# Identity matrix and norm weights loaded ahead of x, and the sums of squares of five norms issued behind the scaled values

## The chip, the cores and the metric

The kernel runs on one core of a Trainium2 chip. The core has a matrix engine (TensorE, PE in the profile), three engines for elementwise work (VectorE or DVE, ScalarE or ACT, GpSimd or POOL) and SyncE (SP), which issues most transfers. Each engine runs its own instructions in order, and an instruction whose input or whose buffer is not ready holds up everything behind it on that engine. The metric is the device time of one execution in microseconds (us), as the median of several runs. Three runs of the kernel before took 1461.05, 1462.23 and 1462.77 us, so its median is 1462.23 us.

## The reference

The program is a decoder trunk of two layers over 256 positions of width 1024, with batch 1.

```python
def rmsnorm(x, g):
    y = xf * lax.rsqrt(jnp.mean(xf * xf, axis=-1, keepdims=True) + EPS) * g
```

Layer 0 normalizes x and multiplies it by one combined input weight. The columns of the product feed a short gated convolution and a gated DeltaNet, which is computed in chunks:

```python
    log_a = -jnp.exp(A_log) * jax.nn.softplus(af + dt_bias)
    beta = jax.nn.sigmoid(bf)
    gc = jnp.cumsum(g, axis=-1)
    decay = jnp.where(tril, jnp.exp(jnp.where(tril, diff, 0.0)), 0.0)
    A = jnp.where(strict, jnp.einsum('bhncd,bhnjd->bhncj', kb, kc) * decay, 0.0)
    M = A + jnp.eye(C)
    u = lax.linalg.triangular_solve(M, vb, left_side=True, lower=True, unit_diagonal=True)
```

After the mixer come an output projection and a residual add, then a dense SwiGLU (width 2816) with its own norm, then a gated embedding add with a norm. Layer 1 is built alike, with differential attention and a convolution module as mixers, and 8 experts (top 2) in place of the dense SwiGLU. A last norm ends it.

## The kernel before

All activations of a layer stand transposed in on-chip memory: 8 tiles of 128 features by 256 positions. Each product is done in pieces: a value v is held as a high part (`..h`, rounded for the fast matrix path) and a low part (`..l`, what the rounding left), and a product of two such values is three matmuls. For weights, SP loads a raw tile (`r_..`), ACT casts it to the high part (`h_..`, L145), and DVE subtracts to get the low part (`l_..`, L146). The casts write into a few buffers in rotation, so a cast waits until the matmuls that used its buffer are done.

A norm is done late: `late_norm_T` (L257) transposes h on PE (`nt_..`, L249), ACT scales each transposed piece by the norm's weight (`x_..h`, L200), DVE makes the low part (`x_..l`, L201). The factor 1/rms of each position is left out there. It is worked out beside it: four `Square` activations per norm with a sum as second output (`sum_sq`, L227; tile `jk_..`), then some small DVE operations (`rsqrt`, L213 to L218; `rq..`), and it is applied to the results of the projection.

The layer-0 mixer runs in this order of use. `in_og` is the projection that gives the output gate and the two small gate inputs af and bf, from four loads of 2 k-tiles each, 96 matmuls of 260 columns. `in_k`, `in_q`, `in_v` (96 matmuls of 256 columns each), `in_cg` and `in_x` follow. From af and bf come beta and the log decay g, by exponentials on ACT and a row of small DVE operations. g goes through a cumulative sum on PE (`pcs`), its exponential (`ec`) and the decay matrices (`pd`, `dec`, and their transposes `pdt`). The key side gives `pk`, and with it the chunk matrices A0 and A1 (one for each half of the positions). Their triangular inverse is built by doubling: `Ti` is set up on DVE, `put` transposes it on PE, ACT copies that to `U`, and then each of six levels does for each half a product `p1`, a masked copy `Ym` on DVE, a product `p2`, an update of U on DVE, a transpose `p3` and a copy to Ti on ACT.

Which instruction stands where on each engine is not the order of the source. A list scheduler goes over the program and lays out each engine's order by its own estimates of times, and it keeps dependences, buffers and the edges that the source sets with `tc.issue_after`. A small edit to the source can thus move instructions far away. The helper `after(*names)` sets such an edge: everything in its block is issued after the named last instruction on its engine; `last["high"]` is the last ACT instruction that made a high part in `split` (L195).

Transfers at the start: SP issues half 0 of x and then the identity (64 KB of `cst`), ACT issues half 1 of x and then the norm weights and other columns (`prm`, 122 KB), and POOL issues a broadcast row of parameters (`row`, L422) and the rest of the constants. Behind its two, SP goes on with the weights, `r_in_og` first.

Of the kernel before, what the change touches and what calls it, by code (L numbers as in the profile page):

```python
# [16 lines left out]
P = 128  # L17
D = 1024
T = 256
NB = 2  # L20
# [63 lines left out]
def trunk_kernel(  # L84
# [3 lines left out]
    ple_w_proj, ple_w_gate, prm_in, row_in, cst_in, oh_in, out, stage=99,  # L88
):
    nc = tc.nc  # L90
    pe, act, dve, pool, sync = nc.tensor, nc.scalar, nc.vector, nc.gpsimd, nc.sync
# [22 lines left out]
    xv = x.rearrange("o (b p) d -> p (o b) d", p=P)  # L114
    cst = cp.tile([P, C_L0], F32, name="cst")
    prm = cp.tile([P, N_COL], F32, name="prm")
    sync.dma_start(h[:, 0, :], xv[:, 0, :])
    act.dma_start(h[:, 1, :], xv[:, 1, :])
    sync.dma_start(cst[:, 0:P], cst_in[:, 0:P])
    act.dma_start(prm, prm_in)  # L120
    ident = cst[:, C_ID : C_ID + P]
    stU = cst[:, C_STU : C_STU + P]
    iota = cst[:, C_IO : C_IO + P]
# [28 lines left out]
    def after(*names):  # L152

        stack = ExitStack()
        for n in names:
            stack.enter_context(tc.issue_after(last[n].ins))
        return stack
# [33 lines left out]
    def parts(shape, tag, name, pool_, bufs=1):  # L191
        return (pool_.tile(shape, F32R, tag=tag + "h", name=name + "h", bufs=bufs),
                pool_.tile(shape, F32R, tag=tag + "l", name=name + "l", bufs=bufs))
# [31 lines left out]
    def sum_sq(ss, name, b, i):  # L225
        junk = s2(f"jk_{name}{b}{i}", [P, 512])
        act.activation(junk, h[:, b, HALF[i]], AF.Square, accum_out=ss[:, i : i + 1])  # L227

    def inv_root(ss, name, n):

        m = gp.tile([P, n], F32, tag=f"ms{n}", name=f"ms_{name}", bufs=2)
        ss = ss.rearrange("q (b i) -> q b i", i=2)
        dve.tensor_tensor(m, ss[:, :, 0], ss[:, :, 1], ADD)
        dve.tensor_scalar(m, m, 1.0 / D, EPS, MUL, ADD)
        return rsqrt(m, n)

    def inv_rms(name, b):

        ss = gp.tile([P, 2], F32, tag="ss", name=f"ss_{name}{b}", bufs=2)
        for i in range(2):  # L240
            sum_sq(ss, name, b, i)
        return inv_root(ss, f"{name}{b}", 1)
# [9 lines left out]
    def gained(xT, gname, k):  # L252
        q = transpose_h(gname, k)
        for j in range(2):
            split(sub2(xT, slice(None), k + j), q[:, j, :], scale=pcol(gname[:3], 8 * int(gname[3]) + k + j))

    def late_norm_T(gname):  # L257


        xT = parts([P, KT, T], "xT", f"x_{gname}", gp, bufs=XT_BUFS)  # L260
        for k in range(0, KT, 2):
            gained(xT, gname, k)
        return xT, [inv_rms(gname, b) for b in range(NB)]

    def halves_norm_T(gname):

# [124 lines left out]
    def ple(i, o, tail=None, mark="", norm=None):  # L391

        xT, r = norm or late_norm_T(f"ple{i}{mark}")
        pieces = LAST_PIECES if tail else PIECES
        pins = {2: [(f"ple{i}", 0, "high"), (f"ple{i}", 0, "low")]} if norm else {}
        banks = proj4(ple_w_gate[i], of(xT), f"pg{i}{mark}", (0, 2), (4,), pieces, pins)

        order = pieces if tail else sorted(pieces)
        gate = {}

        def sigmoid(j):
            if j < len(order):
                b, c, n = order[j]
                gate[j] = s2(f"pg{i}{b}{c}{mark}", [P, n])
                last["sigmoid"] = act.activation(gate[j], banks[b, c], AF.Sigmoid, scale=r[b])

        sigmoid(0)
        for j, (b, c, n) in enumerate(order):
            sigmoid(j + 1)
            g, s = gate[j], slice(c % 512, c % 512 + n)  # L410
            dve.tensor_tensor(g, g, o[b][c // 512][:, s], MUL)
            to = g if tail else h[:, b, c : c + n]
            dve.tensor_tensor(to, g, h[:, b, c : c + n], ADD)
            if tail:
                tail(to, b, c, n)


    def layer0_mixer():
        with tc.tile_pool(name="l0", bufs=1) as lp:
# [16 lines left out]
            def col4(t):  # L436
                return t[:, :, None].to_broadcast([P, 4, P])

            xT, r = late_norm_T("mix0")
            rB, rB2 = spread(r, "mix0")  # L440
            yT = parts([P, KT, T], "xT", "y0", gp, bufs=XT_BUFS)
# [250 lines left out]
    def layer0_ffn():  # L692
        with tc.tile_pool(name="ffn", bufs=1) as lp:
# [4 lines left out]
            for b, n in BLOCKS:  # L698
                copy(b, n)
            xT, r = late_norm_T("ffn0")  # L700
            rB, rB2 = spread(r, "ffn0")
            nt = DFF // P
# [853 lines left out]
```

## Time and profile before

| what | value |
|---|---|
| median of three runs | 1462.23 us (1461.05 to 1462.77) |
| the profiled execution | 1461.34 us |
| span of that execution, first to last instruction | 1459.5 us |
| mean granted clock of TensorE | 0.995 |
| PE busy | 1420.2 us, 97% of the span |
| weight loads of PE | 1202.9 us, 82% |
| DVE busy | 1255.2 us, 86% |
| ACT busy | 1059.0 us, 73% |

The profiled execution took 1.84 us more than its span, and 0.89 us less than the median of the runs. PE is busy nearly all the time, so a gap in its work is what to look for: it has one of 8 us at the start, one of 2 us behind the first transposes, and later ones mostly well under 1 us. Busy time of PE is summed from matmuls whose ends are modelled, and its instructions overlap, so the start times tell more than the lengths. In the rows below, the number in brackets at the end is the engine's idle time before the group, with the engine and instruction that ended it. The numbers behind the tile names are left out by the page, so `p` is p1, p2 or p3, told apart by what they read.

### The profile page before, as it was taken

What the parts mean: (1) busy time and instruction counts of PE and PEld (TensorE: products, weight loads), DVE (VectorE), ACT (ScalarE), POOL (GpSimd) and SP (SyncE); (2) the same over time, 40 slices, a digit from 0 to 9 for tenths busy, and PEclk for the clock granted to TensorE, in tenths of its full rate; (3) what the DMA queues carried; (4) which work ended last, traced back from release to release, by engine and by line L of the source; (5) the groups of instructions that cost most, each with busy time, mean ns of one, the idle gap of its engine ahead of it and who ended that gap; (6) DMA issues with size and microseconds to landing.
All of it is one profiled execution on the core that took longest, in us unless ns stands there. A gap on an engine that the chain in (4) does not pass through costs nothing.

```text
span 1459.5 us, 21991 instructions
## 1 busy us (share of the span) xinstructions
PE 1420.2 (97%) x7726; PEld 1202.9 (82%) x7726; DVE 1255.2 (86%) x1716; ACT 1059.0 (73%) x1441; POOL 5.0 (0%) x14
## 2 busy tenths in 40 slices
PE   7999999999999999999999999999999999999996
PEld 6999899988897888888888678888778888778755
DVE  6868655545789599999999999899999899999997
ACT  6545544446646578898888879788888788888875
POOL 0000000000000000000000000000000000000000
PEclk9999999999999999999999999999999999999998
DMA  9604666555461539999999999999999999999990
GB/s 351 219 8 126 200 197 194 180 186 196 144 200 55 203 110 414 369 375 406 384 401 408 411 382 383 394 371 412 405 414 411 404 369 413 406 410 404 382 340 32
DMA packets 137762, 440.36 MB, mean 302 GB/s; under 512 B 9195, under 2 KB 34316, under 8 KB 123564
## 3 DMA queue, kind: packets, MB, share of 16 engines
q1 hardware_dynamic: 133536, 434.24, 78.3%
q10 hardware_dynamic: 3724, 3.36, 0.7%
q0 software_dynamic: 384, 1.29, 0.3%
q8 instruction: 62, 1.02, 0.3%
q14 instruction: 56, 0.46, 0.1%
HBM read 435.97 MB, written 2.88 MB: 301 GB/s over the span
## 4 chain that ended last, share of the span: by engine, by line
PE 80%; DVE 11%; ACT 4%; issue 3%; DMA 2%; ACTq 0%; POOL 0%; DVEq 0%; POOLq 0%
PE mg L174 16%; PE mu L174 16%; PE y L174 14%; PE fu L174 4%; PE fg L174 4%; PE fd L174 4%; PE mt L174 3%; DVE l L146 3%; PE wo L174 3%; DVE l_d L146 2%; PE pg L174 2%; PE p L174 1%; DVE cc L842 1%; PE in_og L174 1%; PE xg L174 1%
## 5 line engine op out<-in xcount | busy, mean ns | idle before, releaser
L146 DVE TENSOR_TENSOR l<-r_gu,h 128x1024 fp32r<-128x1024 f32 x448 | 518.1, 1218 | 7.7 <-ACT h L145 5.3
L145 ACT CAST h<-r_gu 128x1024 fp32r<-128x1024 f32 x448 | 446.5, 1055 | 30.7 <-PE mu L174 11.7
L146 DVE TENSOR_TENSOR l_d<-r_d,h_d 128x1024 fp32r<-128x1024 f32 x220 | 256.0, 1218 | 11.9 <-ACT h_d L145 11.2
L145 ACT CAST h_d<-r_d 128x1024 fp32r<-128x1024 f32 x220 | 220.2, 1060 | 10.0 <-PE mu L174 4.4
L146 DVE TENSOR_TENSOR l_gu<-r_gu,h_gu 128x1024 fp32r<-128x1024 f32 x44 | 53.8, 1224 | 48.0 <-ACT h_gu L145 48.0
L145 ACT CAST h_gu<-r_gu 128x1024 fp32r<-128x1024 f32 x44 | 46.0, 1049 | 63.8 <-PE fu L174 45.4
L174 PE MATMUL y<-l_d,mh 128*128 128x512 f32 x216 | 70.6, 408 | 2.3 <-DVE l_d L146 2.2
L174 PE MATMUL y<-l_d,mhh 128*128 128x512 f32 x224 | 70.5, 396 | 0.5
L174 PE MATMUL y<-h_d,mhh 128*128 128x512 f32 x224 | 69.5, 391 | 0.0
L174 PE MATMUL y<-h_d,mhl 128*128 128x512 f32 x224 | 69.1, 390 | 0.0
L174 PE MATMUL y<-h_d,mh 128*128 128x512 f32 x216 | 66.9, 391 | 1.3 <-DVE mh L198 1.3
L174 PEld LDWEIGHTS y<-l_d,mh 128*128 128x128 f32 x216 | 37.7, 188 | 21.3 <-DVE l_d L146 15.7
L146 DVE TENSOR_TENSOR l_fd<-r_fd,h_fd 128x1024 fp32r<-128x1024 f32 x22 | 27.0, 1225 | 29.4 <-ACT h_fd L145 28.4
L174 PEld LDWEIGHTS y<-l_d,mhh 128*128 128x128 f32 x224 | 40.9, 188 | 13.5 <-DVE l_d L146 5.7
L174 PE MATMUL fg<-x_ffn0h,h_gu 128*128 128x256 f32 x176 | 49.9, 283 | 0.0
L174 PE MATMUL fg<-x_ffn0h,l_gu 128*128 128x256 f32 x176 | 49.9, 283 | 0.0
L174 PE MATMUL fu<-x_ffn0h,h_gu 128*128 128x256 f32 x176 | 49.9, 283 | 0.0
L174 PE MATMUL fu<-x_ffn0l,h_gu 128*128 128x256 f32 x176 | 49.8, 283 | 0.0
L174 PE MATMUL fu<-x_ffn0h,l_gu 128*128 128x256 f32 x176 | 49.8, 283 | 0.0
L174 PE MATMUL fg<-x_ffn0l,h_gu 128*128 128x256 f32 x176 | 49.8, 283 | 0.0
L174 PEld LDWEIGHTS y<-h_d,mhl 128*128 128x128 f32 x224 | 42.1, 188 | 9.0
L174 PEld LDWEIGHTS y<-h_d,mhh 128*128 128x128 f32 x224 | 41.7, 188 | 9.2 <-ACT h_d L145 0.4
(719 smaller groups left out, 3668.5 us busy)
## 6 DMA issues: line engine op xcount, KB each, us to landing
r_gu<-in_moe_w_gate_up_dram SPq DMA_DIRECT2D x192, 1024.0 KB, 9.0
r_d<-in_moe_w_down_dram SPq DMA_DIRECT2D x110, 1024.0 KB, 8.8
r_gu<-in_moe_w_gate_up_dram SPq DMA_DIRECT2D x64, 512.0 KB, 9.4
r_gu<-in_ffn_w_gate_up_dram SPq DMA_DIRECT2D x44, 512.0 KB, 4.8
r_fd<-in_ffn_w_down_dram SPq DMA_DIRECT2D x11, 1024.0 KB, 4.8
r_wo<-in_ev_w_out_dram SPq DMA_DIRECT2D x4, 1024.0 KB, 5.3
r_pg<-in_ple_w_gate_dram SPq DMA_DIRECT2D x4, 1024.0 KB, 9.8
r_wo<-in_od_w_out_dram SPq DMA_DIRECT2D x4, 1024.0 KB, 5.9
```

The source lines that it names most:

```text
L145: last["wcopy"] = act.copy(wh, raw[:, i : i + step])
L146: last["wsplit"] = dve.tensor_tensor(wl, raw[:, i : i + step], wh.bitcast(F32), SUB)
L174: last["mm"] = pe.matmul(o, a, b, start=start, stop=stop, skip_group_check=shared)
L842: dve.scalar_tensor_tensor(dst[:, sft:], src[:, : T - sft], pcol("dw", (30 - sft) * 4 + c), dst[:, sft:], MUL, ADD)
```

## The change

The two transfers of SP change places, and so do the two of ACT. In `late_norm_T` the sums of squares and the small operations behind them now come under an edge: the Squares are issued behind the last high part of the scaled values. Five norms use it: mix0, ffn0, ple0, mix1, and one in a branch for an overflow of the experts that is not taken in the profiled execution. From L263 on, every line number of the kernel after is higher by one.

```diff
--- before.py
+++ after.py
@@ -114,10 +114,10 @@
     xv = x.rearrange("o (b p) d -> p (o b) d", p=P)
     cst = cp.tile([P, C_L0], F32, name="cst")
     prm = cp.tile([P, N_COL], F32, name="prm")
+    sync.dma_start(cst[:, 0:P], cst_in[:, 0:P])
     sync.dma_start(h[:, 0, :], xv[:, 0, :])
+    act.dma_start(prm, prm_in)
     act.dma_start(h[:, 1, :], xv[:, 1, :])
-    sync.dma_start(cst[:, 0:P], cst_in[:, 0:P])
-    act.dma_start(prm, prm_in)
     ident = cst[:, C_ID : C_ID + P]
     stU = cst[:, C_STU : C_STU + P]
     iota = cst[:, C_IO : C_IO + P]
@@ -260,7 +260,8 @@
         xT = parts([P, KT, T], "xT", f"x_{gname}", gp, bufs=XT_BUFS)
         for k in range(0, KT, 2):
             gained(xT, gname, k)
-        return xT, [inv_rms(gname, b) for b in range(NB)]
+        with after("high"):
+            return xT, [inv_rms(gname, b) for b in range(NB)]
 
     def halves_norm_T(gname):
```

The scheduler lays out the program anew with this edge. The number of instructions on each engine stays the same but for ACT, which has two more loads of an activation table. The order differs only up to the layer-1 mixer; the dense SwiGLU and the experts keep theirs.

On ACT, the start of the program, behind the first exponential: `jk_mix` are the Squares, `x_mix0h` the scaled values, `h_in_og` the weight casts. Before:

```order
L227 ACTIVATE jk_mix_130,ss_mix_129<-h 128x512
L227 ACTIVATE jk_mix_132,ss_mix_129<-h 128x512
L200 ACTIVATE x_mix0h<-nt_mix_0_93,prm 128x256
L227 ACTIVATE jk_mix_151,ss_mix_150<-h 128x512
L200 ACTIVATE x_mix0h<-nt_mix_2_102,prm 128x256
L200 ACTIVATE x_mix0h<-nt_mix_0_93,prm 128x256
L200 ACTIVATE x_mix0h<-nt_mix_4_111,prm 128x256
L200 ACTIVATE x_mix0h<-nt_mix_2_102,prm 128x256
L200 ACTIVATE x_mix0h<-nt_mix_6_120,prm 128x256
L227 ACTIVATE jk_mix_153,ss_mix_150<-h 128x512
L200 ACTIVATE x_mix0h<-nt_mix_4_111,prm 128x256
L145 CAST h_in_og_0_184<-r_in_og_182 128x520
```

After:

```order
L200 ACTIVATE x_mix0h<-nt_mix_0_93,prm 128x256
L145 CAST h_in_og_0_184<-r_in_og_182 128x520
L200 ACTIVATE x_mix0h<-nt_mix_2_102,prm 128x256
L200 ACTIVATE x_mix0h<-nt_mix_0_93,prm 128x256
L145 CAST h_in_og_1_188<-r_in_og_182 128x520
L200 ACTIVATE x_mix0h<-nt_mix_4_111,prm 128x256
L200 ACTIVATE x_mix0h<-nt_mix_2_102,prm 128x256
L200 ACTIVATE x_mix0h<-nt_mix_6_120,prm 128x256
L145 CAST h_in_og_0_218<-r_in_og_216 128x520
L145 CAST h_in_og_1_222<-r_in_og_216 128x520
L200 ACTIVATE x_mix0h<-nt_mix_4_111,prm 128x256
L200 ACTIVATE x_mix0h<-nt_mix_6_120,prm 128x256
```

The four Squares have gone to places 17 to 20, behind the last x_mix0h, and the first weight cast has come forward from place 16 to place 6, with the third and fourth also ahead of the Squares.

On ACT, where the gates of the mixer are made (`sg` the output gate, `bf` and `e` the gate exponentials, `ec` and `dec` the exponentials of pcs and pd). Before:

```order
L458 ACTIVATE sg_319<-in_og_181,rq_158 128x252
L459 ACTIVATE bf<-bf 128x8
L468 ACTIVATE e<-t_337 128x8
L657 ACT_TABLE_LOAD
L657 ACTIVATE sg_318<-sg_318 128x512
L145 CAST h_in_q_0_854<-r_in_q_852 128x1024
L657 ACTIVATE sg_319<-sg_319 128x512
L145 CAST h_in_q_2_858<-r_in_q_852 128x1024
L145 CAST h_in_v_0_1043<-r_in_v_1041 128x1024
L485 ACT_TABLE_LOAD
L485 ACTIVATE ec<-pcs 128x16
L494 ACTIVATE dec_369<-pd_367 128x512
```

After:

```order
L145 CAST h_in_q_0_854<-r_in_q_852 128x1024
L145 CAST h_in_q_2_858<-r_in_q_852 128x1024
L145 CAST h_in_v_0_1043<-r_in_v_1041 128x1024
L658 ACT_TABLE_LOAD
L658 ACTIVATE sg_319<-sg_319 128x512
L145 CAST h_in_v_2_1047<-r_in_v_1041 128x1024
L145 CAST h_in_v_0_1053<-r_in_v_1051 128x1024
L486 ACT_TABLE_LOAD
L486 ACTIVATE ec<-pcs 128x16
L495 ACTIVATE dec_369<-pd_367 128x512
L145 CAST h_in_v_2_1057<-r_in_v_1051 128x1024
L495 ACTIVATE dec_385<-pd_383 128x512
```

Before, two silus behind one table load and three casts stood between the gate exponential `e` and the load for `ec`. Now the first silu, with a load of its own, stands ahead of `bf` and `e` (which need a load again); three casts, a load with the second silu, and two more casts of in_v stand between `e` and the load for `ec`. On PE, pcs moved with it, from within the second half of in_k to behind the first 24 matmuls of in_q.

On PE, the start of the inversion, with the numbers kept in the names (p1_2_0 is the first product of the first level, half 0). Before:

```order
L174 MATMUL in_vb_1062<-x_mix0h_91,l_in_v4_0_1054 128x256
L174 MATMUL in_vb_1062<-x_mix0h_91,h_in_v4_0_1053 128x256
L562 MATMUL put0_602<-cst_73,Ti0_582 128x128 x4
L174 MATMUL in_vb_1062<-x_mix0l_92,h_in_v4_0_1053 128x256
L174 MATMUL in_vb_1062<-x_mix0h_91,l_in_v4_0_1054 128x256
L174 MATMUL in_va_1061<-x_mix0h_91,h_in_v4_0_1053 128x256
L174 MATMUL in_va_1061<-x_mix0l_92,h_in_v4_0_1053 128x256
L174 MATMUL in_va_1061<-x_mix0h_91,l_in_v4_0_1054 128x256
L174 MATMUL in_va_1061<-x_mix0h_91,h_in_v4_0_1053 128x256
L174 MATMUL p1_2_0_626<-U0_585,A0_584 128x64 x4
L174 MATMUL in_va_1061<-x_mix0l_92,h_in_v4_0_1053 128x256
```

After:

```order
L174 MATMUL in_vb_1062<-x_mix0h_91,h_in_v4_2_1057 128x256
L174 MATMUL in_vb_1062<-x_mix0l_92,h_in_v4_2_1057 128x256
L174 MATMUL in_vb_1062<-x_mix0h_91,l_in_v4_2_1058 128x256
L563 MATMUL put0_602<-cst_73,Ti0_582 128x128 x4
L174 MATMUL p1_2_0_626<-U0_585,A0_584 128x64 x4
L174 MATMUL p2_2_0_633<-Ym20_631,Ti0_582 128x64 x3
L563 MATMUL put1_620<-cst_73,Ti1_586 128x128 x4
L174 MATMUL p2_2_0_633<-Ym20_631,Ti0_582 128x64
L174 MATMUL p1_2_1_645<-U1_589,A1_588 128x64 x4
L174 MATMUL in_cga_1335<-x_mix0h_91,h_in_cg0_0_1317 128x256
L584 MATMUL p3_2_0_639<-cst_73,U0_585 128x128 x4
```

Before, put0 stood within in_v, and six matmuls of in_v stood between put0 and p1_2_0 and thirteen between p1_2_0 and p2_2_0. After, in_v is done, and put0, p1_2_0, p2_2_0, put1 and p1_2_1 stand behind one another.

On DVE the order around this place is alike in both kernels: Ti0 (for which put0 waits), then the split of a weight, A1, tt1, then Ym20 (for which p2_2_0 waits). The split there is that of l_in_cg4_2 before, of l_in_x0_2 after.

## Rows read from the trace of the kernel before

**Rows 1.** The page: the span, and the chain of waits by engine.
```profile
span 1459.5 us, 21991 instructions
...
PE 80%; DVE 11%; ACT 4%; issue 3%; DMA 2%; ACTq 0%; POOL 0%; DVEq 0%; POOLq 0%
```

**Rows 2.** Busy time in three stretches: us, then each engine, PEclk, DMA share.
```profile
13.79:28.00 14.21, 14.17 (x100) 13.57 (x100) 12.29 (x34) 10.07 (x16) 0.00 (x0) 0.88 1.05 387
28.00:65.00 37.00, 36.57 (x290) 34.91 (x290) 30.75 (x83) 24.80 (x48) 0.00 (x0) 1.00 0.76 275
75.00:130.00 55.00, 54.93 (x476) 54.33 (x475) 37.71 (x100) 24.74 (x62) 0.00 (x0) 1.00 0.16 46
```

**Rows 3.** ScalarE at the start: start us, length us, line, operation [idle before].
```profile
8.02 0.61 ACT L227 ACTIVATE jk_mix<-h 128x512 f32<-128x512 f32 x1
...
10.30 1.95 ACT L200 ACTIVATE x_mix0h<-nt_mix,prm 128x256 fp32r<-128x256 f32 x5
...
13.11 0.63 ACT L145 CAST h_in_og<-r_in_og 128x520 fp32r<-128x520 f32 x1
...
13.99 1.17 ACT L145 CAST h_in_og<-r_in_og 128x520 fp32r<-128x520 f32 x2
```

**Rows 4.** TensorE at the start, same columns.
```profile
8.19 3.50 PE L249 MATMUL nt_mix<-cst,h 128*128 128x128 f32 x16 [8.19 <-DMA cst<-in_cst_dram]
13.79 0.74 PE L174 MATMUL in_og<-h_in_og,x_mix0h 128*128 128x260 f32 x4 [2.09 <-ACT h_in_og L145]
...
28.05 0.39 PE L174 MATMUL in_ka<-x_mix0h,h_in_k 128*128 128x256 f32 x1
28.27 0.28 PE L174 MATMUL in_ka<-x_mix0l,h_in_k 128*128 128x256 f32 x1
28.39 0.28 PE L174 MATMUL in_ka<-x_mix0h,l_in_k 128*128 128x256 f32 x1
```

**Rows 5.** The tile r_in_og: its transfers, and the time to landing.
```profile
L167 SPq DMA_DIRECT2D r_in_og<-in_ev_w_in_dram x4: 433/509/974, 1.7 to 3.7; - x4
...
DMA to landing us min/median/max: 9.0/9.9/10.9
```

**Rows 6.** ScalarE around the exponentials of the gates.
```profile
36.86 1.05 ACT L145 CAST h_in_v<-r_in_v 128x1024 fp32r<-128x1024 f32 x1 [1.82 <-PE in_kb L174]
37.93 1.28 ACT L485 ACT_TABLE_LOAD   x1
39.23 0.18 ACT L485 ACTIVATE ec<-pcs 128x16 f32<-128x16 f32 x1
39.45 0.60 ACT L494 ACTIVATE dec<-pd 128x512 f32<-128x512 f32 x1
...
46.30 1.05 ACT L145 CAST h_in_v<-r_in_v 128x1024 fp32r<-128x1024 f32 x1 [1.82 <-PE in_qb L174]
```

**Rows 7.** TensorE at the gates and at the start of the inversion.
```profile
37.00 0.61 PE L174 MATMUL pcs<-g,cst 128*128 128x8 f32 x4
...
54.27 1.06 PE L174 MATMUL pk<-acc_k 128*128 128x128 f32 x8
...
65.05 0.63 PE L562 MATMUL put<-cst,Ti 128*128 128x128 f32 x4 [0.37 <-DVE Ti L559]
```

**Rows 8.** VectorE from the norms of k to the first half-level.
```profile
56.95 0.17 DVE L537 TENSOR_SCALAR nk<-nk 128x8 f32<-128x8 f32 x1 [0.93 <-ACT jkk L526]
...
59.26 1.22 DVE L146 TENSOR_TENSOR l_in_cg<-r_in_cg,h_in_cg 128x1024 fp32r<-128x1024 f32 x1
...
61.30 1.12 DVE L554 SCALAR_TENSOR_TENSOR A<-pk,brk,dec 128x128 f32<-128x128 f32 x4
...
64.48 0.42 DVE L559 TENSOR_TENSOR Ti<-Ti,tt 128x256 f32<-128x256 f32 x1
...
67.50 0.42 DVE L575 TENSOR_TENSOR Ym<-p,cst 128x256 f32<-128x256 f32 x1
```

**Rows 9.** ScalarE at the first copy out of the inversion.
```profile
65.71 0.59 ACT L563 COPY U<-put 128x512 f32<-128x512 f32 x1 [1.26 <-PE put L562]
```

## Prediction

> **What bounds the kernel now.** I read the chain of waits first: 80% of it lies on PE, 11% on DVE, 4% on ACT [rows 1]. Then I read busy time by stretch: from 28 to 65 us PE worked 36.57 of 37.00 us, from 75 to 130 us 54.93 of 55.00 [rows 2]. So from 28 us on PE is one stream without gaps through layer 0. What the stream gains or loses there has no later gap to vanish in, and the expert weights are fetched into buffers that this stream sets free. I count a shift at full size. Third came the timelines of PE, ACT and DVE at the start and where the change moves instructions.
>
> At the start PE waits for the identity until 8.19, transposes until 11.69, and then waits 2.09 us for the first weight cast, until 13.79 [rows 4]. That cast came at 13.11 because ACT did four Squares (the first at 8.02) and seven scaled values first [rows 3]. The weights did not hold it: the first transfer was issued at 1.7 and took 9.0, so it was in at 10.7 [rows 5]. Later, the start of the inversion is the one place where PE waited for DVE: put0 began at 65.05, 0.37 after PE was free [rows 7].
>
> **A. The start.** The order on ACT becomes: first scaled value, first cast, two values, a cast, three values, two casts, two values, four Squares, four casts. The first cast now waits for its weights (10.7), a new wait; behind it stand scaled values and casts, which are late by no more than that. The cast takes 0.63 [rows 3], so in_og begins at about 11.35 instead of 13.79: 2.4 us earlier. The other items cost 0.55 a cast (two in 1.17), 0.39 a value (five in 1.95) and 0.62 a Square [rows 3]: two casts are left over after the ones with which PE begins, so by 15.6 half of in_og's weights are cast, the Squares take until 18.1, and the fifth cast ends at 18.7. PE, at 48 matmuls in hand, doesn't reach the fifth cast before 18.7 unless its clock rises early. [...] If the rise comes as late in the program as before, I gain less; if it comes sooner by the shift or more, up to 3.3. Ends: 0 (the weights land at 13 in place of 10.7, since cst and prm now go first) and -3.3. I take -2.4. That cst and prm are in sooner is worth nothing by itself, since the cast is then the later of the two; the exchange costs the halves of x some time, hidden in the same wait.
>
> **B. The gates.** The roots of mix0 come later, since the last Square ends at 18.1 and not at 12.7, and with the two added table loads (1.28 each [rows 6]) the gate exponentials end later. pcs stands later by as much: 22 more matmuls of in_k and 24 of in_q lie ahead of it, at 0.12 us each (28.27 to 28.39 [rows 4]) 5.5 us, and I see no wait there. The wait is one step on. ec and dec now stand behind two casts of in_v; the second needs the buffer of a weight whose last matmul is the one just ahead of pcs (a cast that waits so stands at 46.30, idle 1.82 until in_qb [rows 6]). From there: 0.3 to the start of the cast (estimate), cast 1.05, load 1.28, ec and dec 0.8 [rows 6], that is 3.5 until the transposes of dec can begin. PE has pcs (0.6 [rows 7]), pd (0.5, estimate) and 18 matmuls (2.2) to do in the meantime: 3.2. I take +0.5 with the semaphores between; ends 0 and +2.9 (nothing of the load and the casts covered further on, for both halves).
>
> Of a load the row shows 1.28 us and nothing around it: the cast ahead ends at 37.91, the load runs from 37.93 to 39.21, ec begins at 39.23 [rows 6]. [...] The sum here goes by the row; what a later gate would do is a rival below.
>
> **C. The start of the inversion.** This is the largest loss. Ti0 hangs on DVE: from the norms of k (56.95) over a row of small operations, a split of 1.22 (59.26), A0 (61.30) to Ti0, which ends at 64.90 [rows 8]; pk begins at 54.27 and lasts 1.06 [rows 7], so put0 can begin 9.7 us after the end of pk. That chain is the same after. Before, 78 matmuls of in_q and in_v lay between (9.3 us), and 0.4 was left open; after, 68 (8.1 us), and then in_v is at its end: PE waits 1.6. Then p2_2_0 needs Ym20, which on DVE stands behind the split, A1 and tt1: 1.2 + 1.1 + 0.4 (taken as long as Ym) + 0.4 [rows 8], so p2_2_0 begins 3.1 after put0. Between lie only put0 (0.45 at a pace) and p1_2_0 (0.9): PE waits 1.7 more, where before nineteen matmuls filled it. Then U1: from put to the end of the copy to U are 0.66 + 0.59 [rows 7, 9], with 0.6 of work beside: 0.7 of wait. The next matmul, of in_cg, could fill these gaps but stands behind them. Sum 4.0, less the 0.4 to 0.6 that was open before: +3.4. Ends: +1.5 (only the wait at put0, the rest covered since the chain on DVE runs ahead) and +4.2.
>
> **D. The levels and the other norms.** After the first level one matmul of filler stands in each half-level where p1, Ym (0.42 [rows 8]) and p2 follow each other, fewer than before in the first two. I take +0.3; ends 0 and +1.5. From 75 to 130 us only 0.07 us is open [rows 2], so nothing can be won back there. In the dense SwiGLU's norm and in ple0's the Squares go behind values that PE waits for, and the roots are used later: 0. In mix1 the scheduler puts a weight cast (1.05 [rows 6]) where the first Square (0.62 [rows 3]) stood, ahead of the first scaled value: +0.4. Ends for all three together: -0.6 (a Square that PE no longer waits for) and +1.0.
>
> **Sum.** -2.4 + 0.5 + 3.4 + 0.3 + 0.4 = +2.2 us. Against the profiled execution (1461.34, a span of 1459.5 [rows 1] and 1.84 around it) that is 1463.5. The median of the runs is 0.89 above the profiled one; the changed kernel is measured as a median too, so I put it on the median: 1464.4.
>
> **Rivals.**
> - The inversion starves (slower). A half-level has p1, Ym, p2, the update of U, p3 and the copy to Ti in a row, and PE reaches each step sooner than DVE and ACT. If C is at its upper end (+4.2) and the levels at +1.5, with A as above, B +0.5 and D's norms +0.4: +4.2, 1466.4. It decides for slower as soon as the waits in C and the levels together are over 4.4 (-2.4 + 0.5 + 0.4 + 4.4 = 2.9). For it: the fences show no filler between put0 and in_cg. Against it: later levels have in_cg and in_x as filler.
> - The start pays and the rest is covered. A at -3.3 with the clock risen early, C at +0.6 because DVE has fewer splits to do when it reaches k's norms, B and D 0.2 together: -2.5, 1459.7. For it: all of A is read straight from rows. Against it: DVE's chain to Ti0 does not get shorter.
> - The gates come late. If a table switch holds ACT for twice its row, two more of them make e and then g 2.6 us later (2 x 1.28 [rows 6]), pcs waits for g, and the whole stream with it: about 2.4, with 0.2 to spare (estimate). +4.6, 1466.8. Against it: the load's row with no gap. [...]
> - The change does not do what it says: the first cast is no earlier, since the weights land later behind cst, prm and x. A is 0: +4.6, 1466.8. Against it: the bytes ahead of r_in_og are the same.
>
> **How the numbers follow.** Forecast 0.40 (1463 to 1465.5), starving 0.20, the covered case 0.24, late gates 0.07, no gain at the start 0.09. A change under 0.2% (2.9 us) can't be told from none: faster is below 1459.3, slower above 1465.1. Faster gets about half of the covered case and a little for what I don't see: 0.15. Slower gets most of the starving case (0.16), both cases at 1466.8 (0.15) and a part of the forecast's upper end (0.05): 0.36. The same: 0.49. The range goes from the covered case, 1459.5, to above the late ones, 1467.5.
>
> **What would show it.** A: in_og's first matmul at 11.3 to 11.4, in_k's at 25 to 26 (28.05 before [rows 4]). B: a wait of about half a microsecond ahead of the transposes of dec, none at pcs. C: put0 behind the last matmul of in_v with a wait of 1.6, and about 4 us of open PE time until in_cg. D: less than 0.1 per half-level. The forecast is wrong if PE runs through put0 and p2_2_0 with less than 2 us open, if in_og begins after 12.5, or if the offset between the two traces changes by over 1 us after 130 us.

## The result and the profile after

The changed kernel takes 1469.53 us (median of 5 runs, 1468.51 to 1469.98) against 1461.56 us of the kernel before (5 runs, 1461.05 to 1462.77). The ratio is 1.0052, with a 95% interval from 1.0041 to 1.0063: slower by about 8 us. The prediction was 1464.4 us (+2.2), with a range up to 1467.5, so it had the size wrong and the range too narrow.

The page of the kernel after, its span and its chain of waits by engine:

```profile
span 1467.3 us, 21995 instructions
...
PE 85%; DVE 8%; ACT 3%; issue 2%; DMA 1%; SPq 0%; ACTq 0%; DVEq 0%
```

The profiled execution took 1469.08 us, 1.8 more than its span, as before. PE's share of the chain is 85% against 80% [rows 1], which says little by itself: kernels further down that lose nothing have 84 to 86% too (e2, e8). The stretches by granted clock show where the time is lost (columns as in [rows 2]: us, busy time of PE, PEld, DVE, ACT, POOL, then PEclk, DMA share, GB/s):

```profile
28.00:66.00 38.00, 37.96 (x306) 36.51 (x306) 30.04 (x79) 27.10 (x50) 0.00 (x0) 1.00 0.77 276
66.00:70.70 4.70, 2.35 (x18) 1.79 (x16) 4.67 (x11) 1.63 (x2) 0.00 (x0) 1.00 0.48 169
70.70:87.70 17.00, 16.24 (x76) 16.05 (x77) 7.17 (x17) 3.52 (x8) 0.00 (x0) 0.50 0.04 14
87.70:130.00 42.30, 42.30 (x360) 41.09 (x360) 25.62 (x67) 17.66 (x47) 0.00 (x0) 1.00 0.13 43
```

From 66 to 70.7 us PE is busy for only half of the time, and from 70.7 to 87.7 it runs at a granted clock of 0.50, although it is busy for 16.24 of 17.00 us. Before, the clock was at 1.00 throughout 28 to 65 and 75 to 130 us [rows 2], and in between too; the kernel before from 70 to 88 us:

```profile
70.00:88.00 18.00, 18.00 (x164) 17.93 (x162) 13.19 (x30) 8.18 (x15) 0.00 (x0) 1.00 0.02 7
```

The start of the inversion on PE in the kernel after, with idle time and its cause in brackets:

```profile
66.33 0.28 PE L174 MATMUL in_vb<-x_mix0h,l_in_v 128*128 128x256 f32 x1
68.18 0.63 PE L563 MATMUL put<-cst,Ti 128*128 128x128 f32 x4 [1.57 <-DVE Ti L560]
69.48 1.11 PE L174 MATMUL p<-U,A 128*128 128x64 f32 x8 [0.67 <-ACT U L564]
71.11 1.54 PE L174 MATMUL p<-Ym,Ti 128*128 128x64 f32 x6 [0.52 <-DVE Ym L576]
72.44 1.06 PE L563 MATMUL put<-cst,Ti 128*128 128x128 f32 x4
...
74.18 1.97 PE L174 MATMUL p<-U,A 128*128 128x64 f32 x8 [0.35 <-ACT U L564]
75.91 0.56 PE L174 MATMUL in_cga<-x_mix0h,h_in_cg 128*128 128x256 f32 x1
```

put0 waits 1.57 us for Ti0, p1_2_0 0.67 for U0, p2_2_0 0.52 for Ym20, p1_2_1 0.35 for U1: 3.1 us in all, where put0 waited 0.37 before [rows 7]. The clock falls at 70.7 (1.00 up to there, 0.50 from 70.8 on), when the first two of these waits and the first 0.1 us of the third have passed (in the row from 66.00 to 70.70 PE is idle for 2.35 us); the rest of the waits comes at 0.50 already and can't have caused the fall. From 71.11 on the same work takes 1.7 to 1.9 times as long: six records of p2_2_0 take 1.54 us where eight of p1_2_0 took 1.11, and put1 takes 1.06 where put0 took 0.63.

The start did what the prediction said. On ACT and on PE, answering [rows 3] and [rows 4]:

```profile
8.51 0.47 ACT L200 ACTIVATE x_mix0h<-nt_mix,prm 128x256 fp32r<-128x256 f32 x1 [0.36 <-PE nt_mix L249]
10.37 0.63 ACT L145 CAST h_in_og<-r_in_og 128x520 fp32r<-128x520 f32 x1 [1.39 <-DMA r_in_og<-in_ev_w_in_dram]
...
14.99 0.66 ACT L227 ACTIVATE jk_mix<-h 128x512 f32<-128x512 f32 x1
```

```profile
7.22 3.81 PE L249 MATMUL nt_mix<-cst,h 128*128 128x128 f32 x16 [7.22 <-DMA h<-in_x_dram]
11.05 0.59 PE L174 MATMUL in_og<-h_in_og,x_mix0h 128*128 128x260 f32 x1
...
25.36 0.27 PE L174 MATMUL in_ka<-x_mix0h,h_in_k 128*128 128x256 f32 x1
```

The first cast waits for its weights until 10.37, in_og begins at 11.05 (13.79 before) and in_k at 25.36 (28.05 before): 2.7 us gained. The gain and the loss can be read at two later places, the first gate matmuls of the dense SwiGLU (`fg`) and the attention scores of layer 1 (`asc`); the two numbers ahead of the semicolon are the first and the last start. Before, then after:

```profile
L174 PE MATMUL fg<-x_ffn0h,h_gu x176: 282/283/362, 173.1 to 300.0; 128*128 128x256 f32 x176
```

```profile
L174 PE MATMUL asc<-ak,aq x32: 272/374/480, 439.3 to 465.9; 64*128 64x128 f32 x16, 64*128 64x256 f32 x16
```

```profile
L174 PE MATMUL fg<-x_ffn0h,h_gu x176: 282/283/364, 182.2 to 309.2; 128*128 128x256 f32 x176
```

```profile
L174 PE MATMUL asc<-ak,aq x32: 272/374/480, 447.1 to 473.6; 64*128 64x128 f32 x16, 64*128 64x256 f32 x16
```

The stream is 9.1 us late at fg and 9.2 at its end, and 7.8 at the scores, which is the difference of the spans (1467.3 - 1459.5). So the layer-0 mixer lost 2.7 + 9.1 = 11.8 us behind its start, and something in layer 1 gave back 1.4. In the waits of PE from 400 us on (in total, times, longest) the kernel before had a wait that the kernel after does not have. Before:

```profile
PE asc L174 <- DVE ak L852: 1.5, 1, 1.5
PE cv L174 <- ACT dg L836: 0.5, 1, 0.5
```

After:

```profile
PE cv L174 <- ACT dg L837: 0.5, 1, 0.5
```

### The profile page after: what moved, and what is told of

Its sections match the earlier page's. It is cut to its first block, busy times and chain, and to the rows that moved or that the text cites. A ratio compares the mean times of both kernels' runs of the same rounds, so it can differ in the third digit from the quotient of the medians.

```text
span 1467.3 us, 21995 instructions
## 1 busy us (share of the span) xinstructions
PE 1429.6 (97%) x7726; PEld 1211.1 (83%) x7726; DVE 1256.3 (86%) x1716; ACT 1060.6 (72%) x1443; POOL 4.9 (0%) x14
## 4 chain that ended last, share of the span: by engine, by line
PE 85%; DVE 8%; ACT 3%; issue 2%; DMA 1%; SPq 0%; ACTq 0%; DVEq 0%
PE mg L174 16%; PE mu L174 16%; PE y L174 15%; PE fu L174 4%; PE fg L174 4%; PE fd L174 4%; PE mt L174 3%; DVE l L146 3%; PE wo L174 3%; PE pg L174 2%; PE p L174 2%; DVE l_d L146 1%; PE in_og L174 1%; PE xg L174 1%; PE in_qa L174 1%
## 5 line engine op out<-in xcount | busy, mean ns | idle before, releaser
L146 DVE TENSOR_TENSOR l_d<-r_d,h_d 128x1024 fp32r<-128x1024 f32 x220 | 256.1, 1219 | 11.8 <-ACT h_d L145 11.2
```

Of the source, the lines that this page charges most:

```text
L146: last["wsplit"] = dve.tensor_tensor(wl, raw[:, i : i + step], wh.bitcast(F32), SUB)
```

## The experiments

All were timed beside the kernel before on the same chip; its median was 1461.65 us with the first four, 1462.02 with the second four and 1462.08 with the last four.

**Which part of the change.** Theory: the edge in mix0 moves the gates, this takes the other matmuls away from around put0, PE waits, and the clock falls. Rivals: the later norms, or the transfers. `e1_dma_only` has the four transfers exchanged and no edge:

```diff
-        with after("high"):
+        with after("high") if False else ExitStack():
```

> Only the four transfers change places; no edge in any norm, so the order on every engine is that of the kernel before except for the two DMA issues on SP and on ACT. Theory (the loss comes from the order around put0, which the edge in mix0 makes): the first scaled value and the transposes come a little earlier, but the Squares still stand ahead of the first weight cast, so 0 to -0.7 us against before, about 1461.2, in_og beginning at 13.3 to 13.8. Rival (the exchange of the transfers makes the early start by itself, and the edge only harms): in_og begins before 12 and the time falls by 2 us or more, below 1459.6.

It took 1461.61 us, ratio 0.9998 (0.9989 to 1.0006). The exchange is worth nothing by itself. No run has mix0's edge without the exchange, so what the exchange adds to the early start is not known. `e2_not_mix0` and `e3_mix0_only` split the edge between the norms:

```diff
-        with after("high"):
+        with after("high") if gname != "mix0" else ExitStack():   # e2; e3 has == "mix0"
```

> The exchange of the transfers and the edge in ffn0, ple0, mix1 and the branch norm, but not in mix0; layer 0's mixer stands as before. Theory: no wait beyond 0.7 us at put0, granted clock 1.0 from 20 to 130 us, and the 1.5 us that the changed kernel wins between the first projections of layer 1 and its attention scores (its lead of 9.2 us behind before shrinks there to 7.7) comes from mix1's edge: 1460.0, 1.2 to 1.8 below e1_dma_only. Rival (the 1.5 us come from the shift itself, because some transfer stands still in time and the later kernel no longer waits for it): e2 equals e1 within 0.4 us.

> The exchange of the transfers and the edge in mix0 alone; the other four norms as before. Theory: the whole loss is here. Start 2.6 us earlier, waits of 3.5 to 4 us between the end of in_v and p1_2_1, granted clock 0.5 for about 17 us behind them, in all 9 us lost by the dense SwiGLU, and without mix1's edge no 1.5 us back: 1470.5 to 1471. Rival (the later norms' edges bring nothing, the 1.5 us come from the shift): 1469.5, as the changed kernel.

e2 took 1462.47 us, ratio 0.9998 (0.9990 to 1.0007); e3 1473.79, ratio 1.0073 (1.0061 to 1.0086). The whole loss is in mix0's edge. e2 missed its theory (1460.0); what its trace shows of mix1's edge stands under Layer 1. e3 is 3 us above its theory. Its stretches show why:

```profile
66.00:68.50 2.50, 0.63 (x4) 0.42 (x4) 2.50 (x6) 1.22 (x2) 0.00 (x0) 1.00 0.47 192
68.50:90.00 21.50, 20.36 (x96) 19.99 (x96) 9.09 (x23) 4.70 (x10) 0.00 (x0) 0.52 0.05 13
90.00:92.50 2.50, 2.50 (x14) 2.50 (x13) 1.60 (x4) 0.06 (x1) 0.00 (x0) 0.50 0.00 0
```

Its clock stays at half beyond 92 us and not only to 87.7, though its waits are those of the changed kernel (1.6, 1.0 and 0.5 us). e3's six runs lie between 1469.0 and 1474.8, as if the length of the slow stretch differed between executions; with one trace of the kernel that is not shown.

**Wait or clock.** `e4_dummy_work` fills the waits with matmuls whose results are overwritten:

```diff
                 pu = pz(n, f"put{n}")
+                if n == 0:
+                    for _ in range(4):
+                        mm(pu[:, 0:2, :], A[0][:, 0, :], A[0][:, 0:2, :], True, True)
...
                     p1 = (py, pt)[n](f"p1_{b}_{n}", (P, 4, 64))
+                    if lv == 0:
+                        mm(p1, Ti[n][:, 0, :], Ti[n][:, 0:2, :], True, True)
...
                     p2 = (py, pt)[n](f"p2_{b}_{n}", (P, 4, 64))
+                    if lv == 0 and n == 0:
+                        mm(p2, U[0][:, 0, :], U[0][:, 0:2, :], True, True)
```

> The changed kernel with matmuls added whose results are overwritten: four of 128x256 in f32 on A0 ahead of put0's transposes, one each ahead of p1_2_0, p2_2_0 and p1_2_1, some 3.5 us of work in the places where TensorE waits. Nothing is made ready earlier by it. Theory (the waits cost 3.2 us, and the fall of the granted clock that follows them about 8): the clock stays at 1.0 from 20 to 130 us, the waits are filled with work that is worth nothing, so the 3 us of them stay lost and the 8 of the clock come back: 1461 to 1463. Rival A (the clock falls because the thin products of 64 columns stand without weight matmuls between them, not because of the waits): it falls all the same, 1469 to 1471. Rival B (the clock's fall costs little since the levels wait for DVE and ACT anyway at full clock): clock 1.0, but 1467 to 1469.5.

It took 1461.38 us, ratio 0.9995 (0.9986 to 1.0004): 8 us less than the changed kernel for more work. The clock:

```profile
66.00:70.00 4.00, 4.00 (x30) 3.75 (x28) 3.36 (x9) 0.87 (x2) 0.00 (x0) 1.00 0.44 181
70.00:88.00 18.00, 17.98 (x156) 17.34 (x156) 12.20 (x28) 6.53 (x12) 0.00 (x0) 1.00 0.07 17
```

The scheduler moved some matmuls of in_v behind the added ones, so a part of the filling is real work. `e8_dummy_late` has only the three single matmuls (the order is the changed kernel's), `e11_dummy_first` only the four ahead of put0. The 1.85 us at put0 in what was expected of e8 is counted from the start of the matmul before it (66.33 to 68.18), the 1.57 above is the idle time.

> The changed kernel with one overwritten f32 matmul of 128x256 ahead of each of p1_2_0, p2_2_0 and p1_2_1 and none ahead of put0: the order is that of the changed kernel, the wait of 1.85 us at put0 stays, the three waits behind it (2.2 us together) are filled. Theory (the fall of the clock answers to the whole of the idle time between 66 and 74 us, so to less of it not): clock 1.0, and a time of 1462 to 1463.5. Rival (the wait of 1.85 us at put0 alone takes the clock down): clock 0.5 for 10 us and more behind it, 1467 to 1470.

> The changed kernel with the four overwritten f32 matmuls of 128x256 on A0 ahead of put0 and none behind it: the wait at put0 is filled, the waits at p1_2_0, p2_2_0 and p1_2_1 (2.2 us together) are left, but for four matmuls of in_v that now stand behind put0. Theory (the clock falls only for the whole of the idle time around put0, as e8_dummy_late showed from the other side): clock 1.0, 1461 to 1463. Rival (the thin products without weight matmuls take it down): clock 0.5 for 10 us or more, 1467 to 1470.

The waits of e8 behind its first transposes, up to 175 us, and its clock behind them:

```profile
PE put L567 <- DVE Ti L561: 1.6, 1, 1.6
PE p L175 <- ACT U L568: 0.2, 1, 0.2
```

```profile
70.00:88.00 18.00, 17.95 (x154) 17.04 (x152) 11.70 (x28) 6.87 (x13) 0.00 (x0) 1.00 0.04 12
```

Of e11, the waits behind put0, and its clock:

```profile
PE p L175 <- ACT U L568: 0.7, 2, 0.5
PE p L175 <- DVE Ym L583: 0.5, 1, 0.5
```

```profile
70.00:88.00 18.00, 16.98 (x152) 16.70 (x151) 12.75 (x29) 5.76 (x11) 0.00 (x0) 1.00 0.06 17
```

e8 took 1462.36 us (1.0010, 0.9998 to 1.0023), e11 1460.02 (0.9997, 0.9987 to 1.0006). With the wait of 1.6 us at put0 left and the later ones nearly gone, the clock stays up (1.00 in the row of e8); with the later ones left and the first one filled, it stays up too (1.00 in that of e11). Rival A is out by e11: p1_2_0, p2_2_0, put1 and p1_2_1 run there from 69.0 to 74.8 us with no wide matmul between them. (In e8 the added matmuls stand between them, so it says nothing on that rival.) So in these traces the clock answers to what stands at put0 and behind it together. The added matmuls fill the waits and are work at the same time, so whether it answers to the idle time or to the little work done in that stretch is not separated. It is a near thing: one of e8's ten runs took 1471.25 us with a mean granted clock of 0.988, where the other nine have 0.992 to 0.995, so the clock seems to have fallen in it. One of e11's took 1465.50 us, at a mean of 0.993 that decides nothing.

**Late gates, or missing matmuls.** `e5_q_early` leaves the gates late and brings other matmuls to put0:

```diff
...
+            qT = conv_silu("q", 0)
             A, Ti, U = [], [], []
...
-            qT = conv_silu("q", 0)
```

> The changed kernel with the line qT = conv_silu("q", 0) moved ahead of the set-up of the inversion. The start and the gates stay as late as in the changed kernel (pcs behind 24 matmuls of in_q), but src_q0 and src_q1 now come ahead of the norms of k on VectorE, so the banks of in_q are free and the matmuls of in_cg stand between in_v and put0 and between the steps behind it. Theory (what costs is the lack of other matmuls around put0, not the lateness of the gates): no wait over 0.7 us at put0, clock 1.0 from 20 to 130 us, the early start stays a gain: 1458.5 to 1460.5. Rival (late gates cost time by themselves, since the inversion and what hangs on it come later in the stream and run out of work at their end): waits between 95 and 165 us in place of those at put0, 1463 or more.

It took 1459.53 us, ratio 0.9984 (0.9975 to 0.9993), 10 us below the changed kernel by one moved line. Nothing waits at put0, and the clock stays at 1.00 from 28 to 130 us. The rival has its part: two waits between 95 and 165 us.

```profile
PE in_xa L174 <- DVE src_v L507: 1.1, 1, 1.1
PE in_bga L174 <- ACT cx L674: 1.0, 1, 1.0
```

`e10_q_early_no_mix0` is e5 without mix0's edge, to see what the early q does alone:

> e5_q_early without the edge in mix0: the Squares of mix0 stand ahead of the first cast, as in the kernel before; the exchange of the transfers, the other edges and the early q stay. Theory (the early start is worth 2.6 to 3 us once the inversion has other matmuls around it, and the early q by itself is worth nothing): in_og at 13.8, 1460.2 to 1461.5, that is 1 to 2 us over e5_q_early. Rival (the early q is the gain, and the start nothing): 1459.5, as e5.

It took 1461.55 us, ratio 0.9993 (0.9984 to 1.0002): with in_og at its old place the early q brings nothing that the times can tell from none. The medians put the early start at 2.0 us, the traces at less: in_k begins at 24.7 in e5 and at 28.0 in e10, fg at 172.0 and 172.8, since e5 loses most of the lead in its two waits, and the scores at 436.8 and 437.6. So the start is a gain once it is not lost at put0, of 0.8 us in these two traces up to the scores.

`e6_edge_at_k2` moves mix0's edge one pair of transposes back:

```diff
             gained(xT, gname, k)
+            if k == 2 or gname != "mix0":
+                last["edge"] = last["high"]
-        with after("high"):
+        with after("edge"):
```

> The changed kernel with mix0's edge one step earlier: behind the high parts of the second pair of transposes in place of the fourth. The first two weight casts still stand ahead of the Squares, but the Squares stand ahead of the third and fourth cast; the gates and put0 are back where they stood in the kernel before. Theory: in_og begins at 11.1, 2.3 to 2.7 us of the start are kept, no wait over 0.7 us at put0, clock 1.0 from 20 to 130 us: 1458.7 to 1459.7, faster than both kernels. Rival (the third cast, late behind the Squares, makes TensorE wait within in_og, so that the start gives nothing): in_k begins after 27, 1461 to 1462.

It took 1460.33 us, ratio 0.9990 (0.9981 to 0.9999). The loss is gone with the gates at their old place. But the rival was right on the start: the third cast, behind the Squares, makes PE wait, and the clock is lower behind that wait (0.83 from 18 to 28 us, where the kernel before has 0.99). in_k begins at 28.2, about where it began before (28.05):

```profile
17.07 0.74 PE L174 MATMUL in_og<-h_in_og,x_mix0h 128*128 128x260 f32 x4 [2.28 <-ACT h_in_og L145]
```

```profile
18.00:28.00 10.00, 10.00 (x71) 10.00 (x72) 8.93 (x24) 7.09 (x10) 0.00 (x0) 0.83 1.05 387
```

**Layer 1.** `e7_mix1_only` has the edge in mix1 alone.

> The exchange of the transfers and the edge in mix1 alone. Theory (the wait of the attention scores for VectorE, 1.7 us in the kernel before, goes with mix1's edge, and the stream is 1.4 us earlier from there to the end): 1460.2. Rival (what is won there comes back at the end of layer 1, where the granted clock falls for some microseconds in every kernel so far, since e2_not_mix0 showed the shorter wait but no less time): 1461.6, as before, with the scores 1.4 us earlier and the first expert matmul not.

It took 1460.09 us, ratio 0.9993 (0.9984 to 1.0003). In its trace the wait for the scores is gone, and they begin at 437.7 instead of 439.3, which lasts to the end (its span is 1458.2). In e2 the scores begin at 438.8, with fg at 174.0: 264.8 us from one to the other, where the kernel before needs 266.2. The timings show less: e2 has the same edge and was no faster. The runs of one kernel spread by more than this gain (e7: eight from 1458.5 to 1460.7, three from 1462.3 to 1463.0). The 1.4 us are in both traces, and not established by the times.

**A better version.** `e9_v_cx_early` and `e12_v_first` keep e5's edit and take away its two waits:

```diff
+            vT = conv_silu("v", 2)           # e9: ahead of qk = []; e12: ahead of the levels
...
-            vT = conv_silu("v", 2)
...
+            cx = [s2(f"cx{j}", [P, 2, T]) for j in range(2)]
+            for j, q in enumerate(proj_T(W, 512, xT, "in_cg")):
+                act.copy(cx[j], q)           # ahead of vn, from behind the DeltaNet
```

> e5_q_early, and also vT = conv_silu("v", 2) moved ahead of the products of q and k, and the projection in_cg with its copies cx ahead of the last part of the DeltaNet. e5 lost 1.1 us at in_xa (its banks wait for src_v on VectorE) and 1.0 at in_bga (its banks wait for the copies cx behind the Squares of the output norm on ScalarE). Theory: both waits go, and the stream behind in_bga is 2 us earlier than in e5: 1457.5. Rival (DeltaNet's own chain then sets when its last matmuls come, and the two microseconds come back ahead of the output projection): 1459.5, with a wait between 125 and 165 us.

> As e9_v_cx_early, but with vT = conv_silu("v", 2) ahead of the levels of the inversion, so that in_x is there as filler within them. Theory: as e9, 1457.5, with in_xa beginning before 107 us. Rival (the work on v, 5 us of VectorE, now stands between the steps of the levels and makes TensorE wait there): 1459 to 1461.

e9 took 1457.99 us, ratio 0.9973 (0.9964 to 0.9983), e12 1457.26, ratio 0.9968 (0.9956 to 0.9980). Both beat both kernels. The waits of PE from 8 to 175 us in e12, the whole list:

```profile
PE in_og L174 <- DVE l_in_og L146: 0.3, 1, 0.3
PE in_og L174 <- ACT h_in_og L145: 0.2, 1, 0.2
```

## Why the prediction was wrong, step by step

**A, the start: right.** -2.4 predicted, -2.7 measured (25.36 against 28.05). The first cast waits for weights that landed 8.7 us after an issue at 1.7, as worked out. The open point was when the clock rises. In the kernel before, the matmuls of in_og take 0.42 us each up to 17.94 and 0.28 from 18.32, with a granted clock of 0.62 from 13.79 to 18.20 us and of 1.00 from there to 28.00. In the kernel after they take 0.42 up to 15.63 and 0.28 from 16.21, but the granted clock of its trace reads 1.00 on both sides, so it is not shown that this step is the clock's. In e6 they take 0.28 from 12.00 to 14.51. The end of -3.3 was an estimate. In seven other traces with this start (e3, e4, e5, e8, e9, e11, e12) in_k begins at 24.5 to 25.2, so the gain goes up to 3.5.

**B, the gates: a little too dear.** The two added casts and the table load stand ahead of ec as described, but the transposes of dec began without a wait that is not there before. The answering rows for [rows 6]:

```profile
40.03 1.05 ACT L145 CAST h_in_v<-r_in_v 128x1024 fp32r<-128x1024 f32 x1 [1.82 <-PE in_qb L174]
41.10 1.28 ACT L486 ACT_TABLE_LOAD   x1
42.39 0.18 ACT L486 ACTIVATE ec<-pcs 128x16 f32<-128x16 f32 x1
42.47 0.60 ACT L495 ACTIVATE dec<-pd 128x512 f32<-128x512 f32 x1
```

The load takes 1.28 us, again with nothing around it: the cast ahead ends at 41.08, and ec begins at 42.39. +0.5 was predicted, about 0 measured. This decides against the rival of late gates.

**C, the start of the inversion: the step that failed.** The prediction put it at "Sum 4.0, less the 0.4 to 0.6 that was open before: +3.4. Ends: +1.5 (...) and +4.2." The waits themselves were well read: 1.57 measured at put0 for 1.6, 1.19 between put0 and p2_2_0 for 1.7, 0.35 at p1_2_1 for 0.7, 3.1 in all for 4.0. What failed is that they were priced at their own length. Under A the text reckoned with a clock that is lower at first and rises; under C it did not ask whether the clock would fall behind these waits. It fell, from 70.7 on, behind the first 2.4 us of them, and stood at 0.50 for 17.0 us in the profiled run. If PE's work there takes time as the inverse of the granted clock, it takes at least 8.5 us at 1.00, so up to 8.5 us were lost there (an estimate from the 17.0 and the 0.50). The runs give the same size from the other side: the mixer lost 11.8 us behind its start in the changed kernel. In e8 the order is the same, the gates are as late, and p2_2_0 begins 2.93 us after put0 as it does in the changed kernel, since the added matmuls take the time of the waits that they fill; but the clock is up (1.00 from 70 to 88 us):

```profile
L175 PE MATMUL in_ka<-x_mix0h,h_in_k x16: 274/283/283, 24.6 to 35.2; 128*128 128x256 f32 x16
L175 PE MATMUL fg<-x_ffn0h,h_gu x176: 282/283/364, 174.0 to 301.0; 128*128 128x256 f32 x176
```

From in_k to fg e8 needs 149.4 us, the changed kernel 156.8 (25.4 to 182.2) and the kernel before 145.0 (28.1 to 173.1). So the clock cost 7.4 us. Added to the waits, less what was open before, this is C: 3.1 - 0.4 + 7.4 = 10.1 of the 11.8.

The upper end of C and the slower rival, which had the right sign, failed with it: its own length is no upper price for a wait when the clock falls behind it, as it fell to 0.50 here. The rival's place was right and its mechanism was not. The levels themselves ran at a clock of 1.00 from 87.7 to 130 us without a listed wait.

**D, the other norms: wrong sign, small.** +0.4 was predicted for mix1; its edge took away the wait of the scores (1.5 us), and the stream gained 1.4 there. The prediction looked at the start of mix1 and not at the wait behind it, though the waits of PE listed it. The prediction's own sign for this came: the offset between the two traces changed by over 1 us after 130 us.

**The sum**, with what the runs gave: -2.7 + 0 + 10.1 - 1.4 = +6.0; the difference of the spans is 7.8. What is left, 1.7 us in the layer-0 mixer (11.8 against 10.1), is not the clock's: e8 has it too, at a clock of 1.00 (149.4 - 145.0 is 4.4, of which the waits are 2.7). The +0.3 of D for the levels would be part of it; the runs do not divide it further.

**Rivals.** "The change does not do what it says" and "the gates come late" are out, by A and B. "The start pays and the rest is covered" is what e5, e9 and e12 came near to once other matmuls stood at put0.

## What to carry to other kernels

When a change takes the filler from a chain that TensorE waits for, price the waits twice: at their own length, and at the lower clock that may follow (here 0.50 for 17.0 us), for the work behind them. Here 3.1 us of waits within 8 us, 2.4 of them ahead of the clock's fall, cost about 7 us more. Look at what is left to run beside a serial stretch before moving what feeds it: the same early start stood in a kernel 8 us slower than before with in_v used up, and in kernels 2.5 to 4.8 us faster (e5, e9, e12) with in_cg or in_x brought in by moving a few lines, though not all of that is the start's.

## What the runs showed of the hardware

No wait around put0 was longer than 1.6 us. The clock fell behind 2.4 us of idle time within 66.0 to 70.7 us; with 1.8 us of waits left (e8) or 1.7 (e11) it stayed at 1.00 in the traces. At the start e6 waits once, for 2.28 us up to 17.07, and behind that the mean clock from 18 to 28 us is 0.83. Once down behind put0, it stayed at 0.50 for 17.0 us in one program and beyond 92 us in another with the same waits, while PE was busy 16.24 of 17.00 us with products of 64 columns, transposes and a few wide matmuls. That it stays down so long beside a nearly busy PE was not expected. Why it rose when it did stays open, and so does the part of the transposes in that stretch, which no run takes out. The clock also falls between the mixers and the experts of layer 1 in the ten traces read there, of both kernels and e1 to e8 (a mean of 0.96 to 0.98 from 450 to 530 us; what was expected of e7 calls this place the end of layer 1), for a time that differs between traces. Of the stretch from 515 to 525 us, e2, then e7:

```profile
515.00:520.00 5.00, 5.00 (x19) 4.52 (x20) 3.21 (x20) 3.42 (x6) 0.00 (x0) 0.50 0.00 0
520.00:525.00 5.00, 4.90 (x23) 3.78 (x22) 3.17 (x15) 2.92 (x4) 0.00 (x0) 0.84 0.00 0
```

```profile
515.00:520.00 5.00, 5.00 (x20) 4.04 (x19) 3.73 (x17) 4.49 (x7) 0.00 (x0) 0.66 0.00 0
520.00:525.00 5.00, 4.28 (x30) 3.72 (x30) 4.36 (x19) 2.33 (x3) 0.00 (x0) 1.00 0.00 0
```

That may be why the runs of one kernel spread by some 2 us; no experiment here tested it.
